# One half of each chunk unsplit, in fp32, in the mixers' wide projections; the sixth expert chunk in another room

## The chip, the cores and the metric

The program runs on one core of a Trainium2 chip. The metric is the device time of one execution in microseconds (us), and lower is better. All times below are in us unless ns is written.

## What is computed

The reference is a decoder trunk of two layers on 256 tokens of 1024 features, in fp32. Each layer normalises the tokens, projects them once into four groups, runs a different token mixer in each group, and sends the joined result through an output projection onto the residual. Then comes a channel mixer: a dense SwiGLU in the first layer, eight SwiGLU experts of which each token takes two in the second. A last norm follows.

```python
for layer in range(2):
    h = rms_norm(x, norm1_g[layer])
    u = h @ w_in[layer]                     # 1024 -> 2304 columns, four groups
    y_a = conformer_conv(u[..., :512], ...)       # gated, depthwise conv of width 31
    y_b = pool_mixer(u[..., 512:768], ...)
    y_c = dilated_attention(rope(q), rope(k), v)  # group C
    y_d = diff_attention(rope(q), rope(k), v)     # group D
    x = x + concat([y_a, y_b, y_c, y_d]) @ w_out[layer]
    h = rms_norm(x, norm2_g[layer])
    x = x + (swiglu(h) if layer == 0 else moe_swiglu(h))
return rms_norm(x, final_g)
```

## The kernel before, in words

All weights lie in one array `wst` as chunks of 128 partitions by 2048 fp32 numbers (1 MB each), in the order of their use: 13 chunks for a mixer, 33 for the dense layer, 13 for the second mixer, then 42 for each of eight experts. One queue (SP) loads them in order into raw tiles: nine of them, `raw_p` (`RING`), in rotation. A load waits in that queue until the tile that it overwrites has been read by its last reader, and every later load stands behind it.

**Split products.** TensorE reads fp32 numbers in a reduced form (fp32r) in one go and in full in a slower way. To keep nearly full precision, `halves` (line 178) splits each half of a chunk (1024 columns) into a rounded part `hi`, made by ScalarE (line 190), and a rest `lo`, made by a subtraction (line 191). The subtraction runs on VectorE, or on GpSimd for the halves named in `on_pool`. There are four tiles each for `hi` and `lo`. The tokens are split the same way into `hTh` and `hTl`. A product then takes three matmuls: high by high, low by high, high by low (`moving`, `still`, lines 207 to 213, issued at line 219).

**A mixer.** `enter` (line 308) finishes the layer before: it adds its last products to x, normalises, transposes the tokens to channel-major form into PSUM and splits them into `hTh` and `hTl` (`evict_parts` at line 267, `evict_high` inside `enter`); ScalarE's, VectorE's and (in the first mixer) TensorE's order is written out by hand there. Chunks 0 and 1 feed the convolution. Then `project` (line 409) runs three times, on two chunks each: chunks 2 and 3 (group D's q and k), 6 and 7 (both v), 4 and 5 (group C's q and k). In each chunk j it calls `halves`, and for each half q it issues 2 x 2 products (two blocks of 128 channels, two tiles of 128 tokens) of 128x128 by 128x512, then six taps of the convolution on VectorE (line 401), and whatever the `hooks` hand in: the transposes of group D (line 451), and group D's scores (lines 469 to 479) in the third call. Below, c2 means chunk 2 of a mixer. `halves` puts the second half of c2, c3, c6, c7 and c4 on GpSimd, and both halves of c5 on VectorE:

```python
for j in range(2):
    hs = halves(c + j, () if c + j == c0 + 5 else (1,))
```

After the projections come c8 (the pooling mixer), the rotary products of group C on VectorE (lines 439 to 442), its transposes (line 451), the attention, and the output projection from c9 to c12; c9's second half is subtracted on GpSimd (line 621).

**The experts.** Their first 16 raw tiles are used in the order of the program, chunk by chunk. When the second mixer is done, the rotation is widened (lines 672 to 676): eight more tiles (`raw0` to `raw7`) are made in the room that the mixer's own tiles held, and stand between the first six of the nine and the last three (`LATE = 3`). Four chunks more go into the tiles of `hi` and `lo`. So up to 17 raw tiles and these are filled ahead. Of the eight experts five are taken narrow (64 tokens, chunks used unsplit in full fp32, lines 1004 and 1051) and three wide (128 tokens, split products), in the order narrow, wide, narrow, wide, narrow, wide, narrow, narrow.

Engines that no `manual_schedule` names get their order from a planner, which lays out each engine's list ahead of time by its own costs. On the chip each list then runs strictly in order.

Of the kernel before, what the change touches and what calls it, by code (L numbers as in the profile page):

```python
# [44 lines left out]
LATE = 3  # L45
# [48 lines left out]
def trunk(ctx: ExitStack, tc: tile.TileContext, x_in, wst, cst, par_a, par_l, gains, out):  # L94
# [83 lines left out]
    def halves(c, on_pool=(), between=lambda: None):  # L178

        r = chunk(c) if isinstance(c, int) else c  # L180
        res = []
        for j in range(2):
            w = r[:, j * 1024:(j + 1) * 1024]
            hi = hi_p.tile([P, 1024], F32R, name="hi")
            lo = lo_p.tile([P, 1024], F32R, name="lo")
            eng = nc.gpsimd if j in on_pool else nc.vector
            with ExitStack() as st:
                for ins in behind if split[0] >= FIRST else ():
                    st.enter_context(tc.issue_after(ins))
                nc.scalar.activation(hi, w, AF.Copy)  # L190
                eng.tensor_tensor(out=lo, in0=w, in1=hi.bitcast(F32), op=SUB)  # L191
            split[0] += 1
            if split[0] == HALVES:
                behind.clear()
            res.append((hi, lo))
            if j == 0:
                between()
        return res
# [8 lines left out]
    def moving(ps, xx, w):  # L207

        return (ps, xx[0], w[0]), (ps, xx[1], w[0]), (ps, xx[0], w[1])
# [12 lines left out]
    def cut(pair, *at):  # L222
        return tuple(w[at] for w in pair)
# [84 lines left out]
    def enter(before, c, first):  # L308
# [8 lines left out]
        def evict_high(ps, kk, tt):  # L317

            h = nc.scalar.activation(hTh[:, kk, tt], ps, AF.Copy)
            lows.append(lambda: nc.vector.tensor_tensor(out=hTl[:, kk, tt], in0=ps, in1=hTh[:, kk, tt].bitcast(F32), op=SUB))  # L320
            return h

        with tc.manual_schedule(engines={eng.Activation, eng.DVE} if before else {eng.Activation, eng.DVE, eng.PE}):
# [8 lines left out]
            else:  # L332
                hs = halves(c, (0,), lambda: turned(0, evict_parts))
# [7 lines left out]
            last = turned(1, evict_parts)  # L341
# [3 lines left out]
    def mixer(layer, c0, before):  # L345
# [8 lines left out]
        enter(before, c0, first)  # L354
        if before:
            before[3].close()
        with ExitStack() as held:
# [51 lines left out]
            def project(c, hooks=()):  # L409
# [3 lines left out]
                for j in range(2):  # L413
                    hs = halves(c + j, () if c + j == c0 + 5 else (1,))
                    for q in range(2):
                        w = tuple(h.rearrange("p (k c) -> p k c", k=2) for h in hs[q])
                        products([moving(ps[t], cut(hTp, ALL, 4 * j + 2 * q + k, slice(t * P, (t + 1) * P)), cut(w, ALL, k))
                                  for k in range(2) for t in range(NT)], j + q == 0, j + q == 2)
# [253 lines left out]
        if layer == 1:  # L672

# [465 lines left out]

    done = mixer(0, 0, None)  # L1140
# [132 lines left out]
```

## Time and profile before

| what | value |
|---|---|
| median of 3 runs | 1259.69 us (1259.45 to 1261.0) |
| the profiled execution | 1259.51 us, its span 1257.7 us |
| TensorE (PE) busy | 1196.7 us, 95% of the span |
| VectorE (DVE) busy | 735.8 us, 58% |
| ScalarE (ACT) busy | 591.5 us, 47% |
| GpSimd (POOL) busy | 73.9 us, 6% |
| moved by DMA | 421.98 MB, mean 336 GB/s |
| projections of the first mixer | 26.8 to 75.1 us of the span |
| projections of the second mixer | 325.7 to 373.5 us |
| experts | 436 us to the end |

A shorter profile line of a matmul gives its own length from start to end; matmuls follow each other before the one ahead has ended, so their spacing is what counts. "Idle before" in square brackets is how long the engine stood still ahead of the row, and who ended it. PEld is the loading of weights, which runs beside matmuls.

### The profile page before, as it was taken

How to read it: one execution, taken by the hardware profiler on the slowest of the kernel's cores; microseconds unless marked ns; L12 is line 12 of the kernel's file. 1: busy time of each engine (PE TensorE's matmuls, PEld its weight loads, DVE VectorE, ACT ScalarE, POOL GpSimd, SP SyncE). 2: the span in 40 equal slices, each digit the busy share in tenths (PEclk: the TensorE clock that was granted, in tenths of full speed). 3: DMA queues.
4: the chain of work that ended last, by engine and by line, in shares of the span. 5: the costliest groups of instructions: out<-in, count | busy, mean ns of one | idle time of the engine just before them, and what ended most of it. 6: DMA issues, size and time to landing. Idle time of an engine off the chain costs nothing.

```text
span 1257.7 us, 16634 instructions
## 1 busy us (share of the span) xinstructions
PE 1196.7 (95%) x6154; PEld 790.3 (63%) x6154; DVE 735.8 (58%) x1118; ACT 591.5 (47%) x868; POOL 73.9 (6%) x45
## 2 busy tenths in 40 slices
PE   8789999999888999999999999999999999999975
PEld 6677899998767633588853368874338887333221
DVE  5996655556898521688861188883139887212112
ACT  5374544444556421577741277772137776122112
POOL 3313000000511100000000000000000000000000
PEclk8899999999999999999999999999999999999998
DMA  9532655554532999999999999999999999999995
GB/s 362 213 128 101 230 183 191 184 196 157 193 134 110 413 420 420 419 418 418 417 361 421 419 420 419 419 419 405 420 419 419 420 419 419 415 418 420 420 420 221
DMA packets 60139, 421.98 MB, mean 336 GB/s; under 512 B 6672, under 2 KB 6928, under 8 KB 10256
## 3 DMA queue, kind: packets, MB, share of 16 engines
q1 hardware_dynamic: 60048, 420.82, 83.0%
q8 instruction: 50, 0.82, 0.3%
q14 instruction: 41, 0.34, 0.1%
HBM read 419.75 MB, written 1.05 MB: 335 GB/s over the span
## 4 chain that ended last, share of the span: by engine, by line
PE 58%; DMA 6%; DVE 1%; ACT 1%; issue 0%; POOL 0%; POOLq 0%; ACTq 0%; SPq 0%; DVEq 0%
PE acc L219 19%; PE acc L1004 16%; PE sc L219 9%; PE sc L1051 8%; DMA raw<-wst 6%; PE tr L955 1%; PE tr L1022 1%; PE tr L1071 1%; PE tr L1028 1%; DVE lo L191 1%; PE tr L974 0%; PE tr L965 0%; ACT hi L190 0%; DVE x L1072 0%; DVE raw L915 0%
## 5 line engine op out<-in xcount | busy, mean ns | idle before, releaser
L191 DVE TENSOR_TENSOR lo<-raw,hi 128x1024 fp32r<-128x1024 f32 x351 | 419.9, 1239 | 114.7 <-ACT hi L190 109.9
L190 ACT ACTIVATE hi<-raw 128x1024 fp32r<-128x1024 f32 x370 | 374.0, 1054 | 134.6 <-PE acc L219 61.4
L1004 PE MATMUL acc<-raw,xt 128*64 128x512 f32 x1096 | 251.3, 597 | 5.9 <-DMA raw<-wst 5.6
L1014 DVE TENSOR_TENSOR xs<-xs,acc 64x512 f32<-64x512 f32 x70 | 48.3, 690 | 276.4 <-ACT xs L1013 276.3
L1013 ACT ACTIVATE xs<-acc 64x512 f32<-64x512 f32 x70 | 41.3, 590 | 272.5 <-PE acc L1004 272.5
L1004 PEld LDWEIGHTS acc<-raw,xt 128*64 128x64 f32 x1096 | 73.7, 136 | 150.0 <-issue 131.7
L219 PE MATMUL acc<-lo,xgh 128*128 128x512 f32 x336 | 134.4, 400 | 1.9 <-DVE lo L191 1.6
L219 PE MATMUL acc<-hi,xgh 128*128 128x512 f32 x336 | 132.8, 395 | 0.0
L219 PE MATMUL acc<-hi,xgl 128*128 128x512 f32 x336 | 132.8, 395 | 0.0
L1051 PE MATMUL sc<-raw,ht 128*64 128x512 f32 x552 | 126.3, 594 | 5.0 <-ACT xs L1013 2.6
L219 PE MATMUL sc<-hTh,hi 128*128 128x256 f32 x336 | 93.0, 277 | 0.0
L219 PE MATMUL sc<-hTl,hi 128*128 128x256 f32 x336 | 92.9, 277 | 0.0
L219 PE MATMUL sc<-hTh,lo 128*128 128x256 f32 x336 | 92.9, 276 | 0.0
L1051 PEld LDWEIGHTS sc<-raw,ht 128*64 128x64 f32 x552 | 39.2, 137 | 84.1 <-issue 77.3
L219 PE MATMUL acc<-lo,hTh 128*128 128x512 f32 (+1 forms) x192 | 69.2, 387 | 10.5 <-DVE lo L191 10.4
L219 PEld LDWEIGHTS acc<-lo,xgh 128*128 128x128 f32 x336 | 63.2, 188 | 21.3 <-DVE lo L191 6.4
L219 PEld LDWEIGHTS acc<-hi,xgl 128*128 128x128 f32 x336 | 63.2, 188 | 14.9
L219 PEld LDWEIGHTS acc<-hi,xgh 128*128 128x128 f32 x336 | 63.3, 188 | 14.1
L219 PE MATMUL acc<-hi,hTh 128*128 128x512 f32 (+1 forms) x192 | 70.5, 395 | 0.0
L219 PE MATMUL acc<-hi,hTl 128*128 128x512 f32 (+1 forms) x192 | 70.1, 385 | 0.2
L219 PE MATMUL sc<-hi,hmh 128*128 128x512 f32 x168 | 66.7, 397 | 0.0
L219 PE MATMUL sc<-hi,hml 128*128 128x512 f32 x168 | 66.3, 395 | 0.0
(273 smaller groups left out, 1557.4 us busy)
## 6 DMA issues: line engine op xcount, KB each, us to landing
raw<-wst SPq DMA_DIRECT2D x389, 1024.0 KB, 16.4
raw<-gains SPq DMA_DIRECT2D x4, 512.0 KB, 5.5
raw<-wst SPq DMA_DIRECT2D x4, 512.0 KB, 13.0
hi<-wst SPq DMA_DIRECT2D x4, 512.0 KB, 14.2
lo<-wst SPq DMA_DIRECT2D x4, 512.0 KB, 13.8
pl<-par_l SPq DMA_DIRECT2D x2, 803.5 KB, 9.2
out<-raw SPq DMA_DIRECT2D x4, 256.0 KB, 3.2
x<-x_in SPq DMA_DIRECT2D x2, 256.0 KB, 3.3
```

The lines of the kernel that those rows point to most:

```text
L190: nc.scalar.activation(hi, w, AF.Copy)
L191: eng.tensor_tensor(out=lo, in0=w, in1=hi.bitcast(F32), op=SUB)
L219: nc.tensor.matmul(ps, lhs, rhs, start=start and all(m[0] is not ps for m in seq[:n]), stop=stop and all(m[0] is not ps for m in seq[n + 1:]))
L955: nc.tensor.matmul(pg[q].rearrange("p k c -> p (k c)"), OH[e][:, t], src[:, t, HF[q]], start=t + n == 0, stop=t + n == 2)
L1004: m = nc.tensor.matmul(ps[ROWS[k % 2]], XT[e][:, 4 * j + k], w[:, k % 2], start=j == 0 and k < 2, stop=j == 1 and k > 1)
L1013: nc.scalar.activation(dst[ROWS[0]], ps[ROWS[0]], AF.Copy)
L1014: nc.vector.tensor_add(dst[ROWS[0]], dst[ROWS[0]], ps[ROWS[1]])
L1022: nc.tensor.transpose(ps[:, n, :NARROW], hm[ROWS[0], n * P:(n + 1) * P], ident[ROWS[0], ROWS[0]])
L1028: nc.tensor.transpose(ps[:, n], hm[:, n * P:(n + 1) * P], ident)
L1051: m = nc.tensor.matmul(DP[e][hf][ROWS[n]], HT[i][:, 2 * j + n], half(r, n)[:, HF[hf]], start=s + j == 0, stop=s == NSLAB - 1 and j == 1)
L1071: nc.tensor.matmul(ps, OT[e][:, t], y, start=n == 0, stop=n == 1)
```

## The change

`halves` gets a list `whole`. A half that is named there isn't split: its raw columns are handed on. `project` now asks for that in the first half of each of its chunks (q = 0), with no half on GpSimd, and multiplies it in full fp32 by an unsplit copy of the tokens, `full`: one fp32 product instead of three reduced ones. `enter` writes `full` for the mixers, four more ScalarE copies of 128x512 out of PSUM for each mixer. `full` takes 8 KB in each partition, in a pool `hf` that is opened ahead of the first mixer and closed at the end of the second. The eight tiles raw0 to raw7 are made after that, so raw0 lies in the room of `full`, and raw1 to raw7 where raw0 to raw6 lay. `LATE` becomes 4: the sixth expert chunk in the order of use goes into raw0, and no longer into the sixth of the nine raw tiles.

```diff
-LATE = 3
+LATE = 4
-    def halves(c, on_pool=(), between=lambda: None):
+    def halves(c, on_pool=(), between=lambda: None, whole=()):
             w = r[:, j * 1024:(j + 1) * 1024]
+            if j in whole:
+                res.append((w,))
+                continue
-    def enter(before, c, first):
+    def enter(before, c, first, full=None):
             lows.append(lambda: nc.vector.tensor_tensor(out=hTl[:, kk, tt], in0=ps, in1=hTh[:, kk, tt].bitcast(F32), op=SUB))
+            if full is not None:
+                nc.scalar.activation(full[:, kk, tt], ps, AF.Copy)
             return h
+        def evict_all(ps, kk, tt):
+            last = evict_parts(ps, kk, tt)
+            if full is not None:
+                nc.scalar.activation(full[:, kk, tt], ps, AF.Copy)
+            return last
-                hs = halves(c, (0,), lambda: turned(0, evict_parts))
+                hs = halves(c, (0,), lambda: turned(0, evict_all))
-            last = turned(1, evict_parts)
+            last = turned(1, evict_all)
-        enter(before, c0, first)
+        enter(before, c0, first, full)
-                    hs = halves(c + j, () if c + j == c0 + 5 else (1,))
+                    hs = halves(c + j, whole=(0,))
-                        products([moving(ps[t], cut(hTp, ALL, 4 * j + 2 * q + k, slice(t * P, (t + 1) * P)), cut(w, ALL, k))
-                                  for k in range(2) for t in range(NT)], j + q == 0, j + q == 2)
+                        at = [(4 * j + 2 * q + k, k, t, slice(t * P, (t + 1) * P)) for k in range(2) for t in range(NT)]
+                        if q == 0:
+                            products([[(ps[t], full[:, b, tt], w[0][:, k])] for b, k, t, tt in at], j == 0)
+                        else:
+                            products([moving(ps[t], cut(hTp, ALL, b, tt), cut(w, ALL, k)) for b, k, t, tt in at], False, j == 1)
         if layer == 1:
+            full_only.close()
+    full_only = ExitStack()
+    full = full_only.enter_context(tc.tile_pool(name="hf", bufs=1, reuse_waits="tile")).tile([P, KD, S], F32, name="hTf")
```

## Rows read from the trace of the kernel before

**Rows 1.** The page: TensorE's granted clock and DMA rate in 40 slices.
```profile
PEclk8899999999999999999999999999999999999998
GB/s 362 213 128 101 230 183 191 184 196 157 193 134 110 413 420 420 419 418 418 417 361 421 419 420 419 419 419 405 420 419 419 420 419 419 415 418 420 420 420 221
```
**Rows 2.** The chain that ended last: start, length, what.
```profile
1144.69 3.63 PE sc L1051 x16
1155.73 19.83 DMA raw<-wst
```
**Rows 3.** Busy by stretch: length, PE, PEld, DVE, ACT, POOL, clock, DMA share, GB/s.
```profile
620.00:660.00 40.00, 39.91 (x181) 24.55 (x181) 24.58 (x28) 18.67 (x25) 0.00 (x0) 1.00 0.95 370
```
**Rows 4.** Busy by stretch again: the projections of the two mixers.
```profile
26.80:75.06 48.26, 41.43 (x188) 32.13 (x186) 45.16 (x105) 24.07 (x48) 14.19 (x5) 0.89 0.57 219
325.73:373.49 47.76, 40.81 (x188) 31.09 (x186) 46.84 (x104) 24.30 (x48) 16.94 (x5) 0.96 0.34 122
```
**Rows 5.** PE's waits there: sum, times, longest; then three rows in time.
```profile
PE acc L219 <- DVE lo L191: 6.8, 1, 6.8
...
PE tr L451 <- DVE xs L442: 3.8, 2, 2.9
PE acc L219 <- DVE lo L191: 3.2, 4, 1.9
...
78.83 0.63 PE L451 MATMUL tr<-cs,xs 128*128 128x128 f32 x4 [0.67 <-DVE xs L442]
80.77 0.63 PE L451 MATMUL tr<-cs,xs 128*128 128x128 f32 x4 [1.32 <-DVE nlam L520]
...
379.06 0.63 PE L451 MATMUL tr<-cs,xs 128*128 128x128 f32 x4 [2.63 <-DVE nlam L519]
```
**Rows 6.** Split products one after another (PE in time), and two stretches by clock.
```profile
58.10 0.39 PE L219 MATMUL acc<-hi,hTh 128*128 128x512 f32 x1
58.33 0.39 PE L219 MATMUL acc<-hi,hTl 128*128 128x512 f32 x1
...
41.70:51.95 10.25, 6.17 (x15) 4.82 (x16) 10.25 (x29) 1.06 (x1) 0.00 (x0) 0.50 0.36 122
349.70:352.30 2.60, 2.60 (x8) 2.12 (x7) 2.60 (x7) 0.60 (x1) 0.00 (x0) 0.50 0.00 0
```
**Rows 7.** Full fp32: four products of 256 columns (chain); the narrow experts' group (page).
```profile
408.87 1.74 PE sc L655 x8
...
L1004 PE MATMUL acc<-raw,xt 128*64 128x512 f32 x1096 | 251.3, 597 | 5.9 <-DMA raw<-wst 5.6
```
**Rows 8.** VectorE and GpSimd in time, first mixer.
```profile
28.98 15.21 DVE L401 SCALAR_TENSOR_TENSOR cv<-zp,pl,cv 128x256 f32<-128x256 f32 x22
47.39 4.04 DVE L401 SCALAR_TENSOR_TENSOR cv<-zp,pl,cv 128x256 f32<-128x256 f32 x10
52.49 4.83 DVE L401 SCALAR_TENSOR_TENSOR cv<-zp,pl,cv 128x256 f32<-128x256 f32 x12
...
54.49 6.24 POOL L191 TENSOR_TENSOR lo<-raw,hi 128x1024 fp32r<-128x1024 f32 x1 [12.96 <-ACT hi L190]
```
**Rows 9.** Copies out of PSUM, and the first mixer's entry: ScalarE, VectorE, PE.
```profile
371.95 1.10 ACT L431 ACTIVATE xs<-acc 128x512 f32<-128x512 f32 x2
...
18.84 2.00 ACT L190 ACTIVATE hi<-raw 128x1024 fp32r<-128x1024 f32 x2
...
19.93 2.36 DVE L191 TENSOR_TENSOR lo<-raw,hi 128x1024 fp32r<-128x1024 f32 x2
...
21.45 0.28 PE L219 MATMUL acc<-hTh,lo 128*128 128x256 f32 x1
```
**Rows 10.** SP's queue in time: expert chunks 6, 10 and 11 in order of use.
```profile
401.61 0.33 SPq L159 DMA_DIRECT2D raw<-wst  x1
...
407.06 0.33 SPq L159 DMA_DIRECT2D raw<-wst  x1
412.98 0.33 SPq L159 DMA_DIRECT2D raw<-wst  x1
```

## The prediction, made before the changed kernel was run

> **What bounds the kernel now.** I read the slices first. From the fourteenth slice on the DMA runs at about 420 GB/s; in the mixers it doesn't, and there the granted clock of TensorE drops in some slices [rows 1]. So the experts look bound by the stream of weights, and nothing done in a mixer could matter unless the stream began earlier. The chain of waits says otherwise: from 1155.73 on it is DMA, but what stands ahead of that is PE [rows 2]. The stretch table shows why. Between 620 and 660 PE is busy for 39.91 of 40 us and the DMA falls to 370 GB/s [rows 3]: the wide expert reads its tiles more slowly than they arrive, all are full, and the stream waits for PE. The time lost there is (420 - 370)/420 x 40 = 4.8 us. A stream that has to wait for PE in the middle is set by PE up to that point. Hence whatever lets PE reach the experts earlier by x moves the end by x, as long as the stream starts earlier too, or by no more than those 4.8 us less.
>
> So the question is when PE comes out of the two mixers, and the change works in the projections, the two stretches of 48.26 and 47.76 us [rows 4]. There I read who makes PE wait [rows 5]. In the first mixer one wait of 6.8 us for a `lo` of VectorE; in the second 3.2 us for `lo` (four times) and 3.8 us for the rotary products ahead of the transposes at line 451. After two of these the clock is at 0.50: 6.17 us of PE's work in 41.70 to 51.95 and 2.60 us in 349.70 to 352.30 are done at 1.2 GHz [rows 6], and cost up to half of that more than they would at 2.4 GHz: 3.1 and 1.3 us.
>
> Why VectorE is late is seen in its own rows [rows 8]. It is busy for 45.16 of 48.26 and 46.84 of 47.76 us [rows 4], in strict order, with the taps of the convolution ahead of the `lo` that PE waits for. 22 taps took 15.21 us, 0.69 each, while GpSimd was subtracting; 10 others took 4.04, 0.40 each. The 22 would take 8.9 us at that pace, so 6.3 us were lost to GpSimd.
>
> **What the change removes.** Per mixer, GpSimd's five subtractions in the projections go, and six of the twelve halves are no longer split at all. VectorE keeps six subtractions instead of seven. With the 6.3 us and one subtraction of 1.2 us (2.36 for two, rows 9) taken off, it has 45.16 - 7.5 = 37.7 us of work in the first stretch; in the second it loses no less. That is under what PE has to do (below), so I expect the waits of [rows 5] inside the stretches to go: 6.8 us and, with the clock, 9.9 us in the first mixer; 7.0 and 8.3 us in the second. What is late next is PE itself. The cover for VectorE is then about 5 us; if it isn't there, see the second case below.
>
> **What it adds on PE.** Three reduced matmuls of 512 columns follow each other every 0.23 us (58.10, 58.33) [rows 6], 0.69 us for a product. A full fp32 product of 128x128 by 128x512 stands nowhere in the trace. The nearest row is line 655, the same weights by 256 columns: eight records, two for each product, in 1.74 us [rows 7], 0.2175 for a record. For 512 columns that is 0.435, and 0.87 us for a product. The far end is the group of the narrow experts at line 1004, 597 ns for a record from start to end [rows 7]: if nothing of two records overlapped, 1.19 us. The near end is 0.69, no dearer than now. I take 0.87, since line 655 has the same 128 weights and the same operands from SBUF. A half has four products: 4 x (0.87 - 0.69) = 0.72 us more, six halves 4.4 us per mixer, 8.7 in all (0 to 24).
>
> **What it adds at the entry.** Four copies out of PSUM of 128x512 per mixer; two in a row took 1.10 us [rows 9]. For the first 128 tokens they lie in ScalarE's idle time, but for 0.2 us that I allow in the first mixer, where they run into the squares for the next tokens. For the second 128 tokens they stand ahead of the split of chunk 1. Before, ScalarE began it at 18.84 and VectorE's first `lo` was done at 19.93 + 1.18 = 21.11; PE wanted it at 21.45 [rows 9]. 1.1 us later it comes at 22.2: PE waits 0.75 us. The same in the second mixer. The hand-written list has the transposes' readers in this order, so the planner can't move the copies. I take 0.95 and 0.75 us (0 if PE's list puts the high products first, 2.2 each if all four copies were on the path).
>
> **Loads.** An unsplit half keeps its raw tile until PE has read it, some 3.5 us after the start of its chunk, so the loads behind it on SP's queue leave later or earlier by a few us; their chunks are used tens of us afterwards. The sixth expert chunk was issued at 401.61 [rows 10], when c10 had been split, and all later loads stood behind it. Its new room is free when c5's products are done, and the second stretch of [rows 4] ends at 373.49, some 25 us earlier, and raw1 to raw3 are free once their readers in the attention are through. So chunks 6 to 9 move into a time in which the DMA is idle. What does it bring? The tenth and eleventh still wait for the attention's last transposes and products, at 407.06 and 412.98. Before, the five loads from 401.61 to 407.06 take 5 x 2.5 = 12.5 us at 420 GB/s, until 414.1; now the stream would be ahead by 414.1 - 413.0 = 1.1 us. Since PE, not the stream, is what ends last at 620 to 660, this is worth nothing at the end: the tiles are just full a little earlier. I cost it at 0, and at a gain of 1.1 at most.
>
> **The sum.** First mixer: -9.9 + 4.4 + 0.95 = -4.6. Second: -8.3 + 4.4 + 0.75 = -3.2. Together -7.8 us, against the profiled execution's 1259.51 (span 1257.7 and 1.8 around it), which lies 0.2 under the median: 1251.7, and 1251.9 by the median.
>
> **The rivals.**
> *Waits come back.* The planner writes VectorE's and PE's lists anew by its own costs. The third projection has eight groups of scores, each with a reduction on VectorE that PE needs done to reuse the bank. Of the four waits for `lo` in the second mixer three were short, (3.2 - 1.9)/3 = 0.43 us [rows 5]. If each of the eight groups in both mixers waits so long, 8 x 2 x 0.43 = 6.9 us are given back: 1258.8; with half of them, 1255.3. For it: this projection alone has the reductions beside the taps on VectorE, and its list is strictly in order. Against: 5 us of slack on VectorE.
>
> *GpSimd's last piece falls elsewhere.* c9's second half stays on GpSimd. Before, it held up group C's rotary products, and PE waited 2.63 us at 379.06 and 0.67 and 1.32 in the first mixer (78.83 and 80.77) [rows 5]. Which engine waits isn't fixed: at 54.49 GpSimd took 6.24 us for its piece while VectorE's 12 taps beside it ran at 0.40 each [rows 8]. If VectorE is first this time, up to 2.6 + 2.0 us go as well: 1247.3. The Trainium skill has this as a rule (page "SBUF — State Buffer", section "Who interferes with whom"): GpSimd and a VectorE instruction with two SBUF inputs need the same read port, whoever starts first keeps it for its whole instruction, and the other is blocked. By that rule the trace agrees in both directions, and the order after the change decides.
>
> *Full fp32 costs more than line 655 says.* One mechanism: the two records of a product don't overlap, so 128 weights have to be loaded between them in the open. At 1.19 us for a product the cost is 48 x (1.19 - 0.69) = 24 us instead of 8.7: 1251.9 + 15.3 = 1267.2, slower. It decides from 0.69 + (8.7 + 7.8)/48 = 1.03 us for a product. Against it: at line 655 the weights are loaded as often, and 1.74 us for eight records leave no room for that; for it: 512 columns by 128 weights were never run in full fp32 here.
>
> *The change doesn't do what it says:* the stream, not PE, sets the end, and the products don't count. Then only the loads matter, and these follow the mixer's end as before, so the time differs from the forecast by 1.1 us; I give it no chance of its own.
>
> **How the numbers follow.** Forecast 52%: 1251.9, by itself 1249.5 to 1254.5. Waits come back 22%: 1254.5 to 1259, half of it within 0.2% of before. GpSimd's piece elsewhere 14%: 1246.5 to 1249.5. Fp32 dearer 12%: 1262 to 1270. 0.2% (2.5 us) is about what a measurement of this kernel can tell from no change. Faster 0.52 + 0.11 + 0.14 = 0.77, same 0.11, slower 0.12. The range 1246.5 to 1258.5 leaves out the last case and the end of the second.
>
> **What would show each step.** Right: no row of GpSimd at line 191 in the projections but the one for c9; taps at 0.40 us throughout; no wait over 1 us of PE in them, and no stretch at half clock there; a product of the unsplit half every 0.87 us; stretches of 43 to 45 us instead of 48; four copies a mixer, and a wait of 0.7 us at chunk 1; the sixth load issued near 375 instead of 401.61; DMA below 420 GB/s again where the wide expert ends. Wrong: PE waiting for VectorE between the halves, products over 1 us, or a mixer that is left earlier by 8 us while the end isn't.

## The result

The changed kernel took 1252.3 us in the median of six runs (1249.45 to 1254.85), the kernel before 1259.7 us (1258.17 to 1261.3). The ratio is 0.994 with a 95% interval of 0.9923 to 0.9956: 7.4 us faster, where 7.8 were forecast. The profiled execution took 1251.29 us, with a span of 1249.4 us. Where I cut both traces into stages, at the first product or transpose of each, the time went as follows:

| stage (us) | before | after | difference |
|---|---|---|---|
| start to the first transposes | 9.36 | 8.06 | -1.30 |
| first mixer: entry, up to the projections | 17.44 | 20.56 | +3.12 |
| its projections | 48.26 | 41.31 | -6.95 |
| its attention, up to the dense layer | 46.94 | 48.77 | +1.83 |
| dense layer | 186.23 | 186.22 | 0 |
| second mixer: entry | 17.50 | 18.84 | +1.34 |
| its projections | 47.69 | 41.30 | -6.39 |
| its attention and the routing, up to the first expert product | 62.69 | 61.14 | -1.55 |
| experts and end | 821.6 | 823.2 | +1.6 |
| span | 1257.7 | 1249.4 | -8.3 |

One of the 24 unsplit products of a mixer (0.87 us) is done in the entry already, so 0.87 us of each entry's difference belongs to the projections. The 1.3 us at the start belong to loads that the change doesn't touch. Nor need the 1.6 us at the end be the change's: in the profiled executions of the twelve experiments below that stage took 821.3 to 823.0 us, and 0.85 of the 1.6 us lie behind VectorE's last row, a piece of 7.5 to 9.0 us in those experiments.

The stretches of the changed kernel, in the columns of [rows 4]: length, busy time of PE, PEld, DVE, ACT and POOL, clock, DMA share, GB/s. They are the two projections, a part of the first mixer's attention, and the end of the wide expert.

```profile
28.62:69.93 41.31, 41.31 (x160) 25.12 (x159) 37.93 (x107) 17.83 (x42) 0.00 (x0) 1.00 0.67 253
323.76:365.06 41.30, 41.30 (x160) 25.12 (x158) 37.95 (x107) 17.71 (x42) 0.00 (x0) 1.00 0.46 166
82.36:92.61 10.25, 10.11 (x41) 8.81 (x41) 7.11 (x32) 5.06 (x16) 2.07 (x2) 0.50 0.00 0
605.00:650.00 45.00, 44.91 (x205) 28.67 (x205) 29.66 (x33) 23.05 (x30) 0.00 (x0) 1.00 0.95 363
```

The first two lines answer to [rows 4]. PE is busy without a gap and at full clock, GpSimd does nothing, and VectorE has 37.9 us of work in 41.3, where it had 45.16 in 48.26. The third line is new: in the first mixer's attention PE works for 10.11 us at half the clock, where the kernel before had its half clock inside the projections [rows 6]. The fourth answers to [rows 3]: PE is full and the DMA is below its 420 GB/s, so the stream still waits for PE where the wide expert ends.

The chain that ended last, beside [rows 2] (start, length, what). The scores that stood at 1144.69 stand at 1134.84, 9.9 us earlier. The chain then stays with PE up to 1166.35, where it went over to the stream at 1155.73 before: PE and the stream run nearly level there.

```profile
1134.84 3.63 PE sc L1066 x16
...
1162.98 3.37 PE acc L1019 x15
1166.35 20.11 DMA raw<-wst
```

PE's five largest waits from 8 to 130 us, the first mixer (sum, times, longest), beside [rows 5]:

```profile
PE tr L266 <- DVE xs L258: 2.6, 2, 1.5
PE sc L483 <- DVE nm L489: 1.6, 1, 1.6
PE acc L222 <- ACT hi L193: 1.4, 1, 1.4
PE sc L222 <- DVE lo L194: 0.8, 1, 0.8
PE tr L465 <- DVE xs L456: 0.7, 1, 0.7
```

The wait of 6.8 us for `lo` is gone. What is left in the mixer lies outside the projections: 1.4 us for ScalarE's split of chunk 1 in the entry, and 0.7 and 1.6 us right behind the projections. The rows there show what holds VectorE up (start, length, engine, line, what):

```profile
70.72 1.88 DVE L453 TENSOR_TENSOR xc<-xs,pl 128x128 f32<-128x128 f32 x1
...
79.32 1.22 DVE L194 TENSOR_TENSOR lo<-raw,hi 128x1024 fp32r<-128x1024 f32 x1
80.45 0.29 DVE L489 CUSTOM_DVE_ANT_0 pC<-sc,pl 128x128 f32<-128x128 f32 x1
```

```profile
70.05 2.40 POOL L194 TENSOR_TENSOR lo<-raw,hi 128x1024 fp32r<-128x1024 f32 x1 [53.28 <-PE sc L483]
```

A product that takes 0.28 us elsewhere takes 1.88: it ends with GpSimd's subtraction for c9's second half, the one piece that GpSimd has kept. Everything behind it on VectorE is late, down to c9's first half at 79.32 and the reduction at 80.45, for which PE's scores wait.

The sixth expert chunk's load left SP at 368.0, not 401.61 [rows 10].

### The profile page after: what moved, and what is told of

It is laid out like the page before. It is cut to its first block, busy times and chain, and to the rows that moved or that the text cites. A ratio compares the mean times of both kernels' runs of the same rounds, so it can differ in the third digit from the quotient of the medians.

```text
span 1249.4 us, 16523 instructions
## 1 busy us (share of the span) xinstructions
PE 1202.8 (96%) x6106; PEld 781.0 (63%) x6106; DVE 717.6 (57%) x1116; ACT 583.1 (47%) x864; POOL 38.1 (3%) x35
## 3 DMA queue, kind: packets, MB, share of 16 engines
HBM read 419.75 MB, written 1.05 MB: 337 GB/s over the span
## 4 chain that ended last, share of the span: by engine, by line
PE 60%; DMA 5%; DVE 1%; ACT 1%; issue 0%; POOL 0%; POOLq 0%; ACTq 0%; SPq 0%; DVEq 0%
PE acc L222 19%; PE acc L1019 18%; PE sc L222 9%; PE sc L1066 8%; DMA raw<-wst 5%; PE tr L970 1%; PE tr L1037 1%; PE tr L1086 1%; PE tr L1043 1%; DVE lo L194 1%; PE tr L989 0%; PE tr L980 0%; ACT hi L193 0%; DVE x L1087 0%; DVE raw L930 0%
## 5 line engine op out<-in xcount | busy, mean ns | idle before, releaser
L194 DVE TENSOR_TENSOR lo<-raw,hi 128x1024 fp32r<-128x1024 f32 x349 | 415.2, 1232 | 117.8 <-ACT hi L193 116.2
L193 ACT ACTIVATE hi<-raw 128x1024 fp32r<-128x1024 f32 x358 | 361.6, 1055 | 114.4 <-PE acc L222 48.8
L1028 ACT ACTIVATE xs<-acc 64x512 f32<-64x512 f32 x70 | 41.3, 590 | 273.2 <-PE acc L1019 273.2
L222 PEld LDWEIGHTS sc<-hTh,hi 128*128 128x128 f32 x336 | 63.1, 188 | 0.4
L222 PEld LDWEIGHTS sc<-hTl,hi 128*128 128x128 f32 x336 | 63.1, 188 | 0.4
L222 PEld LDWEIGHTS sc<-hTh,lo 128*128 128x128 f32 x336 | 63.1, 188 | 0.0
```

Of the source, the lines that this page charges most:

```text
L222: nc.tensor.matmul(ps, lhs, rhs, start=start and all(m[0] is not ps for m in seq[:n]), stop=stop and all(m[0] is not ps for m in seq[n + 1:]))
L1028: nc.scalar.activation(dst[ROWS[0]], ps[ROWS[0]], AF.Copy)
```

## The experiments

My theory, from the prediction: GpSimd slows VectorE, VectorE makes PE wait, and both the waits and the half clock behind them go when VectorE has less to do; full fp32 costs 0.87 us a product; the load of the sixth chunk is worth nothing. The rivals: the stream of weights sets the end, so that only the load counts; the number of splits alone matters, not GpSimd; GpSimd alone matters, and the unsplit halves bring nothing; GpSimd's last piece, c9's second half, decides. All runs in one table, each against the kernel before in the same series:

| kernel | median, us | ratio to before | 95% interval |
|---|---|---|---|
| the changed kernel | 1252.3 | 0.9940 | 0.9923 to 0.9956 |
| e1_sixth_back | 1252.4 | 0.9934 | 0.9921 to 0.9947 |
| e2_gpsimd_back | 1263.0 | 1.0024 | 1.0015 to 1.0032 |
| e3_split_vector | 1251.8 | 0.9937 | 0.9921 to 0.9952 |
| e4_all_whole | 1255.2 | 0.9959 | 0.9946 to 0.9972 |
| e5_half_copy | 1249.0 | 0.9916 | 0.9899 to 0.9934 |
| e6_no_copy | 1248.1 | 0.9906 | 0.9889 to 0.9923 |
| e7_c9_vector | 1247.0 | 0.9895 | 0.9879 to 0.9912 |
| e8_first_chunks | 1244.5 | 0.9876 | 0.9859 to 0.9892 |
| e9_first_c9 | 1244.5 | 0.9874 | 0.9859 to 0.9889 |
| e10_half_copy_c9 | 1243.5 | 0.9871 | 0.9855 to 0.9886 |
| e11_split_vector_c9 | 1251.5 | 0.9926 | 0.9912 to 0.9940 |
| e12_no_gpsimd | 1242.8 | 0.9865 | 0.9850 to 0.9880 |

### The sixth load alone

```diff
-LATE = 4
+LATE = 3
```

> The changed kernel with the one edit of the sixth chunk undone: the experts' sixth chunk is loaded where it was loaded before the change, some 33 us later than in the changed kernel (401.61 against 368.04 us). The forecast's reason says that load is worth 0 to 1.1 us, since the first expert product finds its chunks landed either way: a time within 1.5 us of the changed kernel's 1252.3 us, the first expert matmul again near 426 us, and in the stretch where the wide expert ends (605 to 650 us) TensorE still busy throughout. The rival, that the stream of weights sets the end: then the later load takes the gain away, the time is near 1257 to 1260 us, and TensorE waits for weights within the experts.

The time is that of the changed kernel, 1252.4 us. Where the wide expert ends, PE is as full as it was:

```profile
605.00:650.00 45.00, 44.90 (x205) 29.26 (x205) 30.32 (x34) 22.50 (x30) 0.00 (x0) 1.00 0.96 373
```

With the later load the stream has caught up a little less with PE, 373 instead of 363 GB/s, and still waits for it. No worth of the load can be seen in the time, and the rival of the stream falls.

### GpSimd and the unsplit halves, each by itself

First GpSimd back into the projections, with the first halves still unsplit:

```diff
-                    hs = halves(c + j, whole=(0,))
+                    hs = halves(c + j, () if c + j == c0 + 5 else (1,), whole=(0,))
```

> The changed kernel, but in the projections the second half of each chunk is split by GpSimd again (all but the chunk c5, as in the kernel before); the first half stays unsplit in full fp32. It tells apart two things that the change does at once: it takes one split in two away, and it takes GpSimd out of the projections. If VectorE's lateness came from the number of splits alone, the projections stay free of waits at 41.3 us each and the time stays within 1 us of 1252.3 us; VectorE even has less to do. If GpSimd beside VectorE slows VectorE's own operations, the taps take longer than the 0.40 us of the changed kernel (0.69 us in the slow ones of the kernel before), TensorE waits for GpSimd's rest of a half again, the two stretches lengthen by 1 to 2.5 us each and the time is 1254 to 1257 us.

1263.0 us: 10.8 more than the changed kernel and slower than the kernel before. The two stretches:

```profile
29.48:77.12 47.64, 44.69 (x160) 26.35 (x159) 42.09 (x104) 17.90 (x42) 9.04 (x4) 0.93 0.56 216
328.70:375.00 46.30, 43.62 (x160) 25.84 (x158) 41.33 (x104) 17.80 (x42) 9.17 (x4) 0.96 0.42 148
```

They are 6.3 and 5.0 us longer than the changed kernel's, together the whole difference. GpSimd has taken five splits of each mixer over, and VectorE runs four in each of these stretches where it ran six. Yet it has 42.1 and 41.3 us of work where it had 37.9. Its groups from 30 to 75 us (count, busy time, mean in ns) say where from:

```profile
L412 DVE SCALAR_TENSOR_TENSOR cv<-zp,pl,cv 128x256 f32<-128x256 f32 x60 | 28.5, 543 | 0.0
L194 DVE TENSOR_TENSOR lo<-raw,hi 128x1024 fp32r<-128x1024 f32 x4 | 4.8, 1216 | 0.0
L410 DVE TENSOR_SCALAR cv<-zp,pl 128x256 f32<-128x256 f32 x2 | 3.5, 1800 | 0.0
```

The same view of the changed kernel:

```profile
L412 DVE SCALAR_TENSOR_TENSOR cv<-zp,pl,cv 128x256 f32<-128x256 f32 x60 | 24.4, 481 | 0.0
L194 DVE TENSOR_TENSOR lo<-raw,hi 128x1024 fp32r<-128x1024 f32 x6 | 7.2, 1222 | 0.0
L410 DVE TENSOR_SCALAR cv<-zp,pl 128x256 f32<-128x256 f32 x2 | 0.7, 408 | 0.0
```

The 60 taps together are 4.1 us dearer beside GpSimd, and the two first taps 2.8 us. That is more than the two splits (2.4 us) that VectorE has less in this window. So the number of splits alone isn't it. The means hide how the time goes: each of GpSimd's four subtractions in this window holds one instruction of VectorE until it is through, and the other taps follow each other every 0.4 us as usual. Two of the held ones:

```profile
31.31 2.47 DVE L410 TENSOR_SCALAR cv<-zp,pl 128x256 f32<-128x256 f32 x1
33.70 2.62 DVE L412 SCALAR_TENSOR_TENSOR cv<-zp,pl,cv 128x256 f32<-128x256 f32 x1
```

Two taps of 2.62 and 2.56 us are the whole 4.1 us. In the kernel before it was the same: of the 22 taps of [rows 8] that took 0.69 us on the mean, three took 2.56 to 2.64 us each. I had expected 1 to 2.5 us a stretch: the half clock, at 0.93 and 0.96, came back with the waits.

Then the other one alone: the kernel before, nothing unsplit, and VectorE splits all:

```diff
-                    hs = halves(c + j, () if c + j == c0 + 5 else (1,))
+                    hs = halves(c + j)
```

> The kernel before, with one edit: in the projections VectorE splits both halves of every chunk and GpSimd none; nothing is unsplit, there is no full copy of the tokens, and the sixth chunk is where it was. If GpSimd beside VectorE was the whole reason for TensorE's waits, the projections run without waits at TensorE's own 36.8 us each or so (41.3 less six halves at 0.72 us) and without the entry's copies, and the time is 1242 to 1246 us. If VectorE is the bound, as the forecast has it, it has 37.93 us of work as in the changed kernel and six more splits of a half at 1.2 us or so, about 45 us in a stretch: the stretches are 44 to 46 us and the time is 1254 to 1258 us.

1251.8 us, no different from the changed kernel. The stretches are 46.8 and 43.6 us, where the theory said 44 to 46, with VectorE near its limit:

```profile
25.29:72.06 46.77, 43.09 (x190) 33.02 (x188) 42.73 (x108) 24.48 (x48) 0.00 (x0) 0.93 0.61 240
321.00:364.64 43.64, 39.91 (x189) 30.73 (x186) 42.73 (x108) 24.09 (x48) 0.00 (x0) 1.00 0.38 136
```

But the time is 2 to 6 us below my number for it. What the longer stretches cost against the changed kernel, 5.5 and 2.3 us, the entries without copies give back (17.3 and 15.8 us instead of 20.56 and 18.84), and the last stage of the first mixer (47.1 instead of 48.77). That of the second is the same, 61.15 and 61.14.

Put together, the four kernels make a square. Taking GpSimd out of the projections is worth 0.63% with all halves split (1 to 0.9937), and 0.84% with half of them unsplit (1.0024 to 0.994). Leaving halves unsplit costs 0.24% beside GpSimd, and makes no difference without it (0.9937 against 0.994). The gain of this change is GpSimd's leaving. The unsplit halves are one way to make that possible; VectorE could have done the splits too.

### The price of full fp32

```diff
-                    hs = halves(c + j, whole=(0,))
+                    hs = halves(c + j, whole=(0, 1))
...
-                        if q == 0:
-                            products([[(ps[t], full[:, b, tt], w[0][:, k])] for b, k, t, tt in at], j == 0)
-                        else:
-                            products([moving(ps[t], cut(hTp, ALL, b, tt), cut(w, ALL, k)) for b, k, t, tt in at], False, j == 1)
+                        products([[(ps[t], full[:, b, tt], w[0][:, k])] for b, k, t, tt in at], j + q == 0, j + q == 2)
```

> The changed kernel, with both halves of each chunk of the projections unsplit in full fp32, so that no split stands in a projection. It measures the price of an unsplit half where nothing else can hide it: TensorE is the bound of the stretch, and twelve more halves (six in each mixer) change from 24 products at 0.23 us to 8 at 0.862 us, 6.90 against 5.52 us by the spacing of rows or 6.18 by the chunk's half in the changed trace. The forecast's price (0.69 to 0.72 us a half) gives 8.3 to 8.6 us more, 1260.7 us, the first expert matmul near 434.5 us and VectorE mostly idle in the stretches. If a product costs 1.03 us or more, as one rival has it, 12 halves cost 32 us more; if the products are cheaper where no split one stands between them, less than 6 us more.

(The counts of 24 and 8 in that text are those of a chunk, two halves; a half has 12 reduced products or 4 full ones.) The stretches and the attention behind the first:

```profile
29.29:74.63 45.34, 45.34 (x136) 20.72 (x135) 34.11 (x104) 15.86 (x39) 15.59 (x1) 1.00 0.60 232
326.30:371.66 45.36, 45.36 (x137) 20.74 (x135) 33.39 (x102) 12.81 (x36) 2.34 (x1) 1.00 0.42 152
74.63:121.84 47.21, 44.82 (x252) 36.53 (x251) 30.23 (x103) 25.74 (x56) 8.29 (x7) 0.93 0.26 90
```

24 more unsplit products make a stretch 4.03 and 4.06 us longer: 0.168 us each over the 0.69 of a split one, 0.86 us for a full product. From 29.3 to 46.3 us 40 records in a row (20 products) show the same, 17.3/20 = 0.865:

```profile
L222 PE MATMUL acc<-raw,hTf 128*128 128x512 f32 x40 | 17.3, 592 | 0.0
```

So the price is settled, at the forecast's 0.87, and the rival of dear products falls (it decided from 1.03). But of 8.1 us in the stretches only 2.9 reach the median. In the profiled executions the spans differ by 4.3: the two stages behind the projections are 1.6 and 1.4 us shorter, in the first mixer with less half clock (0.93 against 0.90), and the end 1.0. What differs behind the projections is GpSimd's piece of c9, which now stands inside them:

```profile
45.87 15.59 POOL L194 TENSOR_TENSOR lo<-raw,hi 128x1024 fp32r<-128x1024 f32 x1 [28.45 <-ACT hi L193]
```

```profile
327.31 2.34 POOL L194 TENSOR_TENSOR lo<-raw,hi 128x1024 fp32r<-128x1024 f32 x1 [14.15 <-ACT hi L193]
```

In the first mixer GpSimd was the one that was held: 26 taps beside it took 10.39 us, 0.40 each. With the piece out of the way the second mixer's last stage takes 59.8 us, close to the 59.6 that it takes in e7_c9_vector below. In the first, 6.8 us at half clock are left.

### The copies at the entry

```diff
+        def unsplit(ps, kk, tt):
+            if full is not None:
+                nc.scalar.activation(full[:, kk.start:kk.start + 2, tt], ps[:, :2], AF.Copy)
...
-            last = evict_parts(ps, kk, tt)
-            if full is not None:
-                nc.scalar.activation(full[:, kk, tt], ps, AF.Copy)
-            return last
+            if full is None:
+                return evict_parts(ps, kk, tt)
+            h = nc.scalar.activation(hTh[:, kk, tt], ps, AF.Copy)
+            unsplit(ps, kk, tt)
+            return h, nc.vector.tensor_tensor(out=hTl[:, kk, tt], in0=ps, in1=hTh[:, kk, tt].bitcast(F32), op=SUB)
```

> The changed kernel with cheaper full copies at the mixers' entries: only the blocks of tokens that the unsplit halves use (0, 1, 4, 5) are copied, 256 columns instead of 512 for each, and a copy of the second token tile goes ahead of VectorE's read of the same PSUM tile (in the changed kernel it waited 0.76 us for that read). The entries of the run that has no copies (e3_split_vector) are 3.3 and 3.0 us shorter up to the first projection. If the copies are what makes the changed kernel's entries longer, half copies without the wait give some half of that back: 1249.5 to 1251.5 us. If they are hidden, 1252.3 us within 1 us.

1249.0 us, 0.5 below the first range. ScalarE's waits of the first 30 us in the changed kernel, and then in this one:

```profile
ACT hi L193 <- DMA raw<-wst: 4.5, 1, 4.5
ACT hTh L229 <- PE tr L266: 2.4, 1, 2.4
ACT hTf L331 <- DVE hTl L230: 2.3, 3, 0.8
```

```profile
ACT hi L193 <- DMA raw<-wst: 5.5, 2, 5.2
ACT zp L405 <- PE tr L292: 2.5, 1, 2.5
ACT hTh L334 <- PE tr L266: 2.4, 1, 2.4
```

The copy's wait for VectorE's read of the same PSUM tile, three times 0.76 us, is gone from the list. The edit halves the copies as well; no run tells the two apart. In the profiled execution, the fastest of the six, the entries give 2.0 and 0.3 us (17.7 us without and 18.5 us with the early product). Another 1.7 us come from the first mixer's attention (47.06 us), which is at full clock here though the two waits of 0.7 and 1.6 us stand in it.

And with no copy at all:

```diff
-            if full is not None:
-                nc.scalar.activation(full[:, kk, tt], ps, AF.Copy)
...
-                            products([[(ps[t], full[:, b, tt], w[0][:, k])] for b, k, t, tt in at], j == 0)
+                            products([[(ps[t], hTh[:, b, tt].bitcast(F32), w[0][:, k])] for b, k, t, tt in at], j == 0)
```

> The changed kernel without any full copy of the tokens: the unsplit halves of the chunks are multiplied by the tokens' high part alone, read as fp32, so what the low part of the tokens adds to those products is left out; the number and form of the products stay. It gives the price of the copies by itself. If they stand on the path, the entries become as short as in the run without copies (3.3 and 3.0 us less) and the time is 1246.5 to 1249.5 us; at the forecast's price, 0.95 and 0.75 us, it is 1250.6 us; hidden, 1252.3 us. TensorE's stretches stay at 41.3 us in all three.

1248.1 us, within the first range. The entries take 17.2 and 15.7 us, against 20.56 and 18.84 in the changed kernel, 19.7 and 18.0 without the product that belongs to the projections. (In this profile the first mixer's attention is at full clock, and 10.2 us at half clock stand in the second mixer's, from 371.95 on.) But the second entry has something else in it. From its first transposes to the first product of chunk 1 I read, in the fourteen kernels: 11.9 to 12.3 us in nine, 9.98 to 10.3 in four, 10.9 in e12_no_gpsimd. Two rows decide. In the changed kernel (VectorE, then GpSimd):

```profile
304.75 3.43 DVE L194 TENSOR_TENSOR lo<-raw,hi 128x1024 fp32r<-128x1024 f32 x1
```

```profile
304.71 2.39 POOL L194 TENSOR_TENSOR lo<-raw,hi 128x1024 fp32r<-128x1024 f32 x1 [1.33 <-ACT hi L193]
```

And in e6_no_copy:

```profile
300.90 1.22 DVE L194 TENSOR_TENSOR lo<-raw,hi 128x1024 fp32r<-128x1024 f32 x1
```

```profile
300.86 3.53 POOL L194 TENSOR_TENSOR lo<-raw,hi 128x1024 fp32r<-128x1024 f32 x1 [1.33 <-ACT hi L193]
```

Both engines split a half of the same chunk, and start 0.04 us apart, GpSimd first by its row. One of the two is held until the other is through: 3.43 is 2.39 and about one us, 3.53 is 1.22 and 2.3. In seven of the thirteen kernels with this pair, the one before and the changed one among them, it was VectorE, in six GpSimd. With VectorE held, chunk 1 comes at 11.9 us without copies (before, e11) and 12.3 with full ones; with GpSimd held at 10.0 without (e3, e6), and 11.9 to 12.0 with full ones (e2, e4). So the copies cost the second entry 0.4 us in the one case and 2.0 in the other, and of the 2.3 us between the profiled second entries of e6 and the changed kernel most is this change of sides. The same pair stands at the dense layer's entry. There GpSimd starts 0.44 to 0.50 us ahead, and in all thirteen kernels VectorE is the one that is held, for 3.4 us. In the first entry, where VectorE was held nowhere near so long, the copies cost 2.3 (against before) to 2.5 us (against e6).

### GpSimd's last piece

```diff
-                hs = halves(c0 + 9 + n, () if n else (1,))
+                hs = halves(c0 + 9 + n)
```

> The changed kernel with the second half of chunk c9, which GpSimd still splits just behind the projections, given to VectorE. The third rival of the forecast says this piece decides: in the changed kernel it took 2.40 us on GpSimd and one of VectorE's products beside it 1.88 instead of 0.28 us. If that delay of 1.6 us in each mixer reaches TensorE, the time falls by 1.5 to 3 us, to 1249.3 to 1250.8 us. If it is covered (TensorE waits only 0.65 and 0.71 us there), VectorE's own 1.2 us for the split takes its place and the time stays at 1252.3 us within 1 us.

1247.0 us, 5.3 below the changed kernel and more than expected. The projections, the attention behind them, and the time in which the changed kernel was at half clock:

```profile
29.67:70.99 41.32, 41.32 (x160) 25.13 (x159) 37.93 (x107) 17.84 (x42) 0.00 (x0) 1.00 0.64 244
70.99:116.55 45.56, 42.66 (x252) 34.25 (x251) 32.23 (x105) 26.30 (x58) 9.14 (x7) 1.00 0.28 102
82.00:92.00 10.00, 8.34 (x50) 6.45 (x50) 8.48 (x37) 5.23 (x15) 2.07 (x2) 1.00 0.00 0
```

The attention of the changed kernel in the same view:

```profile
69.93:118.70 48.77, 46.26 (x253) 38.32 (x251) 31.96 (x104) 26.34 (x58) 11.59 (x8) 0.90 0.27 90
```

3.2 us less, and none of it from idle time: PE was idle for 2.51 us there and is idle for 2.90 now. Its busy time fell by 3.6 us, because the clock is at full speed throughout. At the scores PE waits 0.5 us now instead of 1.6, and 0.2 instead of 0.7 at the transposes ahead of them:

```profile
PE sc L483 <- DVE nm L489: 0.5, 1, 0.5
PE tr L505 <- DVE pD L545: 0.2, 1, 0.2
PE tr L465 <- DVE xs L456: 0.2, 1, 0.2
```

The second mixer's last stage is 1.6 us shorter, there through the waits alone. And the runs lie closer: 1246.7 to 1247.2 us in five, with mean clocks from 0.994 to 0.997, where the changed kernel's six spread over 5.4 us, with 0.986 to 0.996. Its fastest, at 0.996, took 1249.45 us, which suggests that about half of the 5.3 us is clock that the changed kernel loses in most runs and not in all. The rival of the last piece was right that this piece holds up VectorE, and PE behind it; its price counted the waits alone.

### Nearer to even, and all together

Half as many unsplit halves, with VectorE splitting the rest, and with the copies of e5_half_copy for blocks 0 and 1 alone:

```diff
-                    hs = halves(c + j, whole=(0,))
+                    hs = halves(c + j, whole=(0,) if j == 0 else ())
...
-                        if q == 0:
+                        if q + j == 0:
...
```

> Only half as many unsplit halves: of the two chunks of each projection the first chunk's first half is unsplit, the second chunk is split in both halves by VectorE, GpSimd has none, and only the tokens' blocks 0 and 1 are copied at the entries. TensorE has 41.3 less three times 0.69 us, 39.2 us a stretch, VectorE 37.9 and three splits of 1.22 us more, 41.6 us: the two are nearly even. If the sum of the engines' work is what counts, the stretches stay near 41.5 to 42.5 us and the cheaper copies give 1 to 2 us an entry: 1248 to 1251 us. If VectorE so close to the bound brings TensorE's waits and half clock back (42.7 us of work took 46.8 us in e3_split_vector), the stretches are 44 us or longer and the time is 1252 to 1256 us.

1244.5 us, below both ranges.

```profile
26.10:67.42 41.32, 40.61 (x176) 28.01 (x175) 39.80 (x105) 21.89 (x46) 0.00 (x0) 1.00 0.69 262
319.90:360.40 40.50, 40.42 (x175) 27.55 (x173) 40.33 (x106) 20.73 (x45) 0.00 (x0) 1.00 0.43 145
```

PE 40.6 and VectorE 39.8 in 41.3 us, 40.4 and 40.3 in 40.5. All 48 products lie inside the stretches here, so they answer to 42.2 us in the changed kernel and are 0.9 and 1.7 us shorter. PE hardly waits, and the entries have a quarter of the copies. Near the bound isn't over it: with 42.73 of work in e3_split_vector it was.

Then four kernels that put these edits together. The first takes e8_first_chunks and the edit of e7_c9_vector:

> The kernel with half as many unsplit halves (e8_first_chunks), and c9's second half split by VectorE as in e7_c9_vector: GpSimd splits nothing from the entry's first chunk to the last two chunks of the mixer. Alone the two edits gave 1244.45 and 1246.96 us. If GpSimd's piece behind the projections is what brings TensorE's wait for the scores and the half clock into the attention, whatever the projections look like, the time is 1239.5 to 1242.5 us. If e8_first_chunks owes its time to an attention that is already clear of it (it shows 3.4 us of half clock there against 10.2 in the changed kernel), nothing is left to gain: 1243.5 to 1245 us.

1244.5 us: nothing is left to gain. That isn't because the attention was clear already: 6.8 us at half clock stand in the first mixer's, in e8_first_chunks (two times 3.4) as here (from 83.79 on). PE waits for other work of VectorE instead (two waits for `pm`, in the attention, where e8_first_chunks has one of 1.1 us):

```profile
PE acc L603 <- DVE pm L579: 3.0, 2, 1.8
PE acc L222 <- DVE lo L194: 1.8, 2, 1.0
```

The second takes e5_half_copy and the edit of e7_c9_vector:

> The changed kernel with the half copies of e5_half_copy and c9's second half on VectorE as in e7_c9_vector. If the two prices are independent (3.3 us for the copies, 5.3 us for c9), the time is 1243 to 1244.5 us; if both only take the same half clock away (the profiled run of e5_half_copy shows none in the attention), it is 1246 to 1247.5 us. Beside e11_split_vector_c9 it also tells what the unsplit halves themselves are worth once GpSimd is out of the way.

1243.5 us, the first range. That the two prices are independent isn't shown by it, though: the 1.7 us that e5_half_copy's profile gained in the attention and the 3.2 us of e7_c9_vector are the same half clock, and here GpSimd was the one held at the second entry, which takes 17.3 us where e5_half_copy's took 18.5. The whole first mixer is at full clock.

```profile
26.00:68.14 42.14, 42.14 (x163) 25.47 (x161) 38.32 (x107) 18.95 (x43) 0.00 (x0) 1.00 0.70 275
68.14:113.67 45.53, 42.64 (x253) 34.25 (x252) 32.21 (x105) 26.31 (x58) 9.16 (x7) 1.00 0.27 98
```

The third takes e3_split_vector and the edit of e7_c9_vector, with nothing unsplit:

> The kernel before with no unsplit half, VectorE splitting both halves of every chunk of the projections as in e3_split_vector, and c9's second half too; the sixth chunk is where it was. It takes the idea of full fp32 away and keeps the idea of no GpSimd. VectorE is the bound of the projections (42.7 us of work in 46.8 us), and c9 gives it 1.2 us more right behind them. If GpSimd is the whole story, it gains the 5 us that c9 gave the changed kernel: 1246 to 1248 us, and the unsplit halves are worth no more than 2 or 3 us. If VectorE's queue is what decides, the added split makes it later still and the time stays at 1251 to 1253 us.

1251.5 us, no better than without that edit. PE's waits for VectorE's splits are there as in e3_split_vector (six of them, 7.4 us), seven up to the first expert:

```profile
PE acc L219 <- DVE lo L191: 7.8, 7, 1.6
```

At the second entry VectorE was held here and GpSimd in e3_split_vector (17.5 and 15.8 us), so up to 1.7 us of gain may be hidden. The fair partner is e7, where VectorE was held too. Here the unsplit halves earn their price: with c9 on VectorE the kernel with them takes 1247.0 us (e7), the one without 1251.5. So the theory that GpSimd is the whole story falls at this point. It holds for the change as it was made, not for what can be built on it.

The fourth is e9_first_c9 with the entry's piece on VectorE too:

```diff
-                hs = halves(c, (1,))
+                hs = halves(c)
...
-                hs = halves(c, (0,), lambda: turned(0, evict_all))
+                hs = halves(c, (), lambda: turned(0, evict_all))
```

> e9_first_c9 with the first chunk's second half (second mixer) or first half (first mixer) at the entry split by VectorE too, so that GpSimd splits only the last two chunks of a mixer. In the changed kernel the entry's piece took 2.39 us on GpSimd and VectorE's seven splits beside it took 1.54 us each on the mean against 1.22 elsewhere. If that reaches TensorE, 0.5 to 2 us below e9_first_c9; if VectorE's own 1.2 us an entry takes its place, the same within 1 us or up to 1.5 us above.

The first of these two edits serves the dense layer's entry as well, so GpSimd has left that too, and the dense layer takes 185.1 us where it took 186.0 to 186.3 in all the other kernels.

1242.8 us, the lowest median of all. Against e9_first_c9 (0.9865 and 0.9874) and e10_half_copy_c9 (0.9871) the intervals overlap, so these three can't be told apart. All are faster than both kernels, by 15.8 to 17.5 us against the one before and 7.8 to 9.5 against the changed one (ratios of 0.9874 to 0.9865 beside 0.9940).

## Why the prediction was right, point by point

**What bounds the kernel.** Right. PE's earlier arrival at the experts moved the end: the first expert product came 9.9 us earlier, the end 8.3. The stream still waits for PE at the end of the wide expert (363 GB/s), and with the sixth load in its old place nothing changed.

**The projections.** Right in every row. VectorE was forecast at 37.7 us of work and has 37.93; 60 taps took 24.4 us, 0.41 each; no wait, no half clock, no GpSimd. (The 6.3 us lost to GpSimd were right as a sum; they lay in three held taps, not in 22 slow ones.) The stretches are 41.3 us, 42.2 with the product that is done early, a little under the 43 to 45 of the text.

**Full fp32.** Right: 0.86 to 0.865 us a product, forecast 0.87 from line 655 [rows 7].

**The entry's copies.** This term was mis-sized in the first mixer: 0.95 was forecast, 2.3 us is what the stage shows (3.12 less 0.87). The step that failed is "for the first 128 tokens they lie in ScalarE's idle time", and that two copies cost 1.10 us: three of the copies wait 0.76 us each for VectorE, which reads the same PSUM tile, and PE's wait at chunk 1 was 1.4 us, not 0.75. In the second mixer 0.75 was forecast and 0.47 measured (1.34 less 0.87), but that was the case in which VectorE was held anyway; in the other it would have been 2.0.

**Where the half clock went.** This is what the sum didn't have. The forecast took 3.1 us of clock out of the first mixer's projections, and they are gone there. But the attention behind, at full clock before, has 10.25 us of half clock now, and PE's busy time in it rises from 42.69 to 46.26 us. Its waits fall from 4.25 to 2.51, so the stage is 1.83 longer. In the first mixer the edits of the stages sum to -2.0 us, not -4.6.

**What made up for it.** The second mixer gained 6.6, not 3.2. Its stretch is 42.2 us with the early product, where the sum came to 43.9 (47.76 - 8.3 + 4.4). And 1.55 us came in the last stage, which the sum left alone: the wait of 2.63 [rows 5] became waits of 0.7 and 1.6, and the 3.4 us at half clock behind it, from 379.6 to 383.0, are gone. So the right total came of two halves, each wrong by some 3 us, with opposite signs. That the errors cancelled is luck: which attention falls to half clock changes from kernel to kernel (below), and this is one execution of each.

**The rivals.** Waits didn't come back in the projections. GpSimd's last piece held VectorE up again, as before, so that rival didn't happen; but its price, 4.6 us for both mixers by the text, is near what e7_c9_vector then showed (5.3), there about half by the clock. The Trainium skill (page "SBUF — State Buffer", section "Who interferes with whom") says that issue order decides who blocks. The traces agree that one of the two is blocked, and show both sides of it, but with the same order in the rows, GpSimd first by 0.04 us, either engine was the one that was held, seven times and six. Where GpSimd was ahead by 0.44 us or more, the traces agree with the rule thirteen times of thirteen.

**What stays open.** When an attention falls to half clock. The changed kernel, e1_sixth_back, e2_gpsimd_back, e5_half_copy and e6_no_copy have the same two waits of 0.7 and 1.6 us there at the same two lines in both mixers, ten attentions in all. In four of them 10.2 us at half clock follow (the first mixer of the changed kernel and of e1, the second of e2 and of e6), in one 3.4 us (the second of e1), in five none. So it isn't the mixer that decides. With the shorter waits of e7_c9_vector and e10_half_copy_c9 it was none of four; in e9_first_c9, e11_split_vector_c9 and e12_no_gpsimd, with c9 on VectorE but longer waits for `pm`, the first mixer fell again, for 6.8 us each. That fewer and shorter waits keep the clock up fits all of these; the exact condition isn't shown. Nor is it shown what decides which of the two engines is held at the second entry.

## What to carry to other kernels

An engine that helps out on the side can cost more than it takes over: price the helper by what the main engine's own rows cost beside it (here one tap of 2.6 us instead of 0.48 for each subtraction), and try the change without the other half of the idea, since "no helper" alone gave the same time here as the whole edit. When a stretch is cleared of waits, look at the stage behind it before adding up: what was late there (one instruction held for 1.6 us, then, in some runs, a half clock worth 3.6 us) can be the next thing to take out, and was worth 5 us more here. And copy only what is read: half of the copied tokens had no reader.

## What the runs showed of the hardware

A full fp32 product of 128x128 by 128x512 takes 0.865 us in a row of them, two records each, against 0.69 us for the three reduced ones: a split product is only 0.17 us cheaper on PE, and costs 1.22 us of VectorE and 1.05 of ScalarE for every four. GpSimd and VectorE, each subtracting 128x1024 from SBUF, don't share: one takes its usual time (2.39 or 1.22 us) and the other is stretched to 3.43 or 3.53. Beside GpSimd even the first taps, with scalar operands and one tile, took 1.13 and 2.47 us instead of 0.41 (line 410 in e2_gpsimd_back). When GpSimd started 0.44 us or more ahead, VectorE was the one held in thirteen kernels of thirteen; at 0.04 us it was either. And a kernel's spread can be a symptom: 5.4 us over six runs whose mean clocks range from 0.986 to 0.996, 0.5 us over five with 0.994 to 0.997.
